# Layer 1's attention scores in split parts, with its side work set later, in a two-layer decoder trunk

## The chip, the cores and the metric

One core of a Trainium2 chip runs the whole program in one launch. The metric is the device time in microseconds (us), as the median over runs. TensorE is called PE here, as in the profile (PEld is its loading of weights), VectorE DVE, ScalarE ACT, GpSimd POOL and SyncE SP.

## The reference

A trunk of two layers on x of 256 tokens by 2048 features, in float32. Each layer is a token mixer and a gated MLP, each behind an RMS norm. Layer 0's mixer is attention in which every query attends causally to its own block of 256 keys; layer 1's is latent attention (MLA), and only that is changed:

```python
cq = rms_norm(h @ wq_a, g_qa)                       # rank 512
q = (cq @ wq_b).reshape(B, S, H, NOPE + RD)         # 16 heads of 128 + 64
q_nope = rms_norm(q[..., :NOPE], g_qn)
q_rope = rope(rms_norm(q[..., NOPE:], g_qr), pos, RD)
kv_a = h @ wkv_a
ckv = rms_norm(kv_a[..., :512], g_kva)
k_rope = rope(rms_norm(kv_a[..., 512:], g_kr), pos, RD)   # one for all heads
kv = (ckv @ wkv_b).reshape(B, S, H, NOPE + VD)
k_nope = rms_norm(kv[..., :NOPE], g_kn)
v = kv[..., NOPE:]
s = (q_nope @ k_nope.T + q_rope @ k_rope.T) * scale       # per head, causal
o = softmax(s) @ v
```

## The kernel before, in words

All weights stream once from HBM, in 1464 pieces of 128x512 (some 128x576). SP loads them four at a time into `raw`; ACT casts each to `whi` (fp32r) and DVE makes the remainder `wlo` = raw - whi (L111, L112). A product of two float32 operands is then three fp32r products: high by high, low by high, high by low. A plain float32 product is two passes on PE.

The program is a list of *quanta*, one for each weight piece: a quantum is the products of that piece, six of 128x512 where tokens are the rows (`tok_major`, L250), twelve of 128x256 where features are (`feat_major`, L276 to L278). The order is written out by hand: `at(q, f)` hangs side work behind the products of quantum q, `first_in` hangs work ahead of that. Each engine gets its instructions in the order of this list and runs them strictly in that order, except that PE loads weights ahead. At the start of quantum q the cast and the remainder of piece q + 3 are issued; `whi` and `wlo` have five buffers each.

Layer 1's attention takes four groups of four heads. Group 0 has its pieces in the order queries, rotary queries (second half), keys, values; groups 1 to 3 in the order keys, queries, values, four pieces each. The quanta of group 1 are 836 to 847, of group 2 848 to 859, of group 3 860 to 871; then the output projection begins. For queries and for keys a `Heads` object does, from the quantum q of the last piece on:

- `evac`: ACT copies both halves of the tokens from PSUM into a tile `qk` (two buffers in all)
- `squares`: DVE sums the squares of each head (L394); `rstd`: POOL takes the power -1/2
- `scaled`: DVE multiplies by it (L425); `turned`: PE transposes two heads (L473) into a tile `tp`, of which there are two in PSUM, shared with the probabilities' transposes
- `turned_out`: ACT copies `tp` with the gain into a part of a big tile `room` (L484)

Before, these stand at q, q+1 and q+2, q+3, q+5 and q+6, q+9 and q+10; and queries and keys have two places each in `room`, which takes the buffer of the norm's tile `h`.

A `Head` computes at its quantum the scores on PE: for the first 128 queries by the first 128 keys (columns 0 to 127 of a PSUM tile `sc`), and for the second 128 queries by all 256 keys. In layer 1 each is a plain float32 product (L510) followed by two fp32r products of the rotary parts (L515). In layer 0 (`parts=True`) the second product is in three fp32r products (`three`, L488 to L490), the first plain (L505). Then `biased` adds the mask and takes the maximum (DVE, L521), `exps` (ACT, L530) a quantum later, `normal` (DVE, L537, L539) two later, `turn` (PE, L547) and `turned` six later, `values` (PE, L572, L573) nine later. The heads of a group come three quanta apart, beginning 11 after the queries' (in group 0: keys') last piece.

The rotary queries of heads 8 to 15 (`rotary_queries(1, ...)`) are scaled, rotated in eight DVE steps and turned at offsets from quantum 827 given by a list.

Of the kernel before, what the change touches and what calls it, by code (L numbers as in the profile page):

```python
# [10 lines left out]
F32 = mybir.dt.float32  # L11
# [6 lines left out]
P = 128  # L18
# [32 lines left out]
BY_TOKEN, BY_FEATURE = (8, 8), (24, 56)  # L51

H_START = 8


class Stream:
# [66 lines left out]
def trunk(ctx: ExitStack, tc: tile.TileContext, a, out):  # L123
# [104 lines left out]
    def at(q, f, *args):  # L228
        side.setdefault(q, []).append((f, args))
# [51 lines left out]
    class Norm:  # L281
# [86 lines left out]
    class Heads:  # L368


        def __init__(self, state, n_heads, dh, gain, rot, tabs, scale, gain_column=None):
            self.gain_column = gain_column
# [26 lines left out]
        def squared(self):  # L399

            self.sq = []
            for t in range(NT):
                sq = att_pool.tile([P, 16 * 32], F32, name="ro2", bufs=2)
                nc.scalar.activation(sq, self.x[:, t].rearrange("p n d -> p (n d)"), AF.Square)
                self.sq.append(sq.rearrange("p (n d) -> p n d", n=self.n))

# [13 lines left out]
            nc.gpsimd.tensor_tensor(self.r, ms, mhalf[:, : NT * n], op=ALU.pow)  # L420

        def scaled(self, t):
            if self.gain_column is not None or self.gain is None:
                r = self.r[:, t * self.n : (t + 1) * self.n]
                nc.vector.tensor_tensor(  # L425
                    self.x[:, t], self.x[:, t], r[:, :, None].to_broadcast([P, self.n, self.dh]),
                    op=ALU.mult,
                )
                return
            g = gains[:, self.gain : self.gain + self.dh]  # L430
            for i in range(self.n):
                c = t * self.n + i
                nc.vector.scalar_tensor_tensor(
                    self.x[:, t, i], self.x[:, t, i], self.r[:, c : c + 1], g,
                    op0=ALU.mult, op1=ALU.mult,
                )
# [38 lines left out]
                    )  # L475
            pair["tp"] = tp

        def turned_out(self, dst, pair, i0):
            o = dst[:, i0 : i0 + 2, :].rearrange("p a s -> p (a s)")
            if self.gain_column is None:  # L480
                nc.scalar.copy(o, pair["tp"])
            else:
                c = self.gain_column
                nc.scalar.activation(o, pair["tp"], AF.Copy, scale=par[:, c : c + 1])  # L484

    def three(o, w_hi, w_lo, m_hi, m_lo, start, stop):

        mm(o, w_hi, m_hi, start=start, stop=False)  # L488
        mm(o, w_hi, m_lo, start=False, stop=False)  # L489
        mm(o, w_lo, m_hi, start=False, stop=stop)  # L490


    class Head:
# [4 lines left out]
        def scores(self):  # L498
            sc = ps_sc.tile([P, 512], F32, name="sc")
            qT, kT, i = self.qT(), self.kT(), self.i  # L500
            self.sc = sc
            if self.parts:

                (q0, q1), (k0, k) = qT, kT
                mm(sc[:, :P], q0[:, i], k0[:, i], start=True, stop=True)  # L505
                three(sc[:, P : 3 * P], q1[:, 0, i], q1[:, 1, i], k[:, 0, i], k[:, 1, i], True, True)
                return
            for q0, n, c in ((0, P, 0), (P, S, P)):
                o = sc[:, c : c + n]
                mm(o, qT[:, i, q0 : q0 + P], kT[:, i, :n], start=True, stop=self.rope is None)  # L510
                if self.rope is not None:

                    qr, kr = self.rope()
                    for part in range(2):
                        mm(o, qr[:, q0 : q0 + P], kr[:, part, :n], start=False, stop=part == 1)  # L515

        def biased(self):
            self.s = att_pool.tile([P, 3 * P], F32, name="s", bufs=3)
# [63 lines left out]
        def plan(self, q, q_values, q_turn=None):  # L582


            q_turn = q_turn or q + 6
            at(q, self.scores)
            at(q, self.biased)
            at(q + 1, self.exps)
            at(q + 2, self.normal)
            first_in(q_turn, 1, self.turn)  # L590
            first_in(q_turn, 1, self.turned)
            first_in(q_values, 0, self.values)
            first_in(q_values, 0, self.parted)
# [17 lines left out]
            att_pool.tile([P, 2, 512], F32R, name="v"), att_pool.tile([P, 512], F32, name="v1"),  # L611
        )

    def queries_out(dst, tp, i0):
# [4 lines left out]
        nc.scalar.copy(hi, src[:, :, 1])  # L619
        nc.scalar.copy(q0[:, i0 : i0 + 2], src[:, :, 0])  # L620
        nc.vector.tensor_tensor(lo, src[:, :, 1], hi.bitcast(F32), op=ALU.subtract)

    def keys_out(dst, tp, i0):

        k0, k = dst
        src = tp.rearrange("p (a s) -> p a s", a=2)
        hi, lo = k[:, 0, i0 : i0 + 2], k[:, 1, i0 : i0 + 2]
        nc.scalar.copy(hi, src)
        nc.scalar.copy(k0[:, i0 : i0 + 2], src[:, :, :P])
        nc.vector.tensor_tensor(lo, src, hi.bitcast(F32), op=ALU.subtract)  # L630

    def evac_parts(state, key, scale):
        v0, v1 = env[key]
# [14 lines left out]
            else:  # L648
                nc.scalar.activation(dst, src, AF.Copy, scale=scale()[:, t : t + 1])

    def plan_heads(q, hs, key, step, out=None, late=0, wide=False):

        at(q, hs.evac)
        if wide:
            for t in range(NT):
                for i in (0, 2):
                    at(q + 1 + 2 * t + i // 2, hs.squares, t, range(i, i + 2))
                at(q + 8 + t, hs.scaled, t)
            at(q + 5, hs.rstd)
            for i0 in (0, 2):  # L660
                pair = {}
                q1 = q + 11 + i0 // 2
                at(q1, lambda p=pair, i0=i0: hs.turned(env[key], p, i0))
                at(q1, lambda p=pair, i0=i0: hs.turned_out(env[key], p, i0))
            return
        for t in range(NT):
            at(q + step * (1 + t), hs.squares, t)
        at(q + step * 3, hs.rstd)
        for t in range(NT):
            at(q + step * (5 + t) + late * (1 + t), hs.scaled, t)  # L670
            at(q + step * (5 + t) + late * (2 + t), hs.rotate, t)
        for i0 in (0, 2):
            pair = {}
            q1 = q + step * 9 + i0 // 2 + 2 * late
            at(q1, lambda hs=hs, p=pair, i0=i0, key=key: hs.turned(env[key], p, i0))
            if out is None:
                at(q1, lambda hs=hs, p=pair, i0=i0, key=key: hs.turned_out(env[key], p, i0))
            else:
                at(q1, lambda p=pair, i0=i0, key=key: out(env[key], p["tp"], i0))

    at(-1, n1.scaled, 0)
    at(9, load_constants)
# [1 line left out]
    for g in range(4):  # L684
        for kind in "qkv":
# [13 lines left out]
            if kind == "v":  # L699
                at(q, evac_parts, state, ("v", g), lambda: n1.rstd)  # L700
                q_v = q
            else:
                hs = Heads(state, 4, P, G_Q if kind == "q" else G_K, 32, (tab, T_MC, T_MS), lambda: n1.rstd)
                plan_heads(q + (0 if g else 15 if kind == "q" else 9), hs, ("qT" if kind == "q" else "kT", g), 1,
                           queries_out if kind == "q" else keys_out, 1)
                q_k = q
        for i in range(4):
            hd = Head(
# [378 lines left out]
    at(q + 13, kr_turn)  # L1087

    def mla_tiles(g):
        i = 4 * (g % 2)  # L1090
        env["qT", g] = env["room"][:, i : 4 + i]
        env["kT", g] = env["room"][:, 8 + i : 12 + i]
        i = 4 * (g % 3)
        env["v", g] = env["room"][:, 16 + i : 20 + i].rearrange("p (t c) s -> p t (c s)", t=NT)

    for g in range(4):
        for kind in "kqv" if g else "qrkv":
            if kind == "r":
                rotary_queries(1, (6, 10, 12, 15, 16, 17, 18, 20, 21, 23, 24, 25, 26, 28, 40))
                continue  # L1100
            state = {}
            for kt in range(4):
# [3 lines left out]
            if kind == "v":  # L1106
                at(q, evac_values, state, ("v", g), None)
            else:
                q_q = q
                hs = Heads(state, 4, P, None, 0, None, (lambda: cq["scale"]) if kind == "q" else None,  # L1110
                           C_GQN if kind == "q" else C_GKN)
# [143 lines left out]
```

## Time and profile before

| | |
|---|---|
| median of 3 runs | 2088.53 us (2088.42 to 2088.66) |
| profiled execution: its own time | 2088.55 us |
| its span | 2086.5 us |
| mean granted PE clock | 1.00 |
| PE busy | 2079.9 us (100%) |
| PEld busy | 2012.3 us (96%) |
| DVE busy | 1406.8 us (67%) |
| ACT busy | 1133.2 us (54%) |
| mean HBM read | 186 GB/s |

The span runs from the first to the last instruction in the trace; the execution's own time has some 2 us around it. Matmuls overlap on PE, so the durations in the rows are longer than the distance of their starts: what a product costs is read from starts. "idle before" is how long an engine stood ahead of an instruction, and the arrow names what ended that.

### The profile page before, as it was taken

The numbers are of one execution on the slowest core, as the hardware profiler recorded it, in microseconds if no ns is written. First come the engines' busy times: TensorE is split into PE (matmuls) and PEld (weight loads), VectorE is DVE, ScalarE is ACT, GpSimd is POOL, SyncE is SP. The second block draws the span as 40 slices with busy tenths as digits, with TensorE's granted clock in tenths as the row PEclk, the third lists the DMA queues.
The fourth block names the chain that finished last, engine by engine and source line by source line (L and its number), as shares of the span: only waits on it lengthen the run. The fifth ranks groups of instructions, "written<-read, shape, count | busy, mean of one in ns | idle before, by whom it ended". The sixth has DMA issues, their size and how long they took to land.

```text
span 2086.5 us, 42075 instructions
## 1 busy us (share of the span) xinstructions
PE 2079.9 (100%) x16716; PEld 2012.3 (96%) x16716; DVE 1406.8 (67%) x3012; ACT 1133.2 (54%) x2199; POOL 46.1 (2%) x35
## 2 busy tenths in 40 slices
PE   9999999999999999999999999999999999999999
PEld 7888889999999999999999889999999999999999
DVE  6777776776666766655556886776676666755554
ACT  6555555555555555545455666655555555544443
POOL 0000000000000000000000110000000000000000
PEclk9999999999999999999999999999999999999999
DMA  7454445455555555555554533555555555555553
GB/s 270 166 182 173 168 164 200 185 192 192 199 187 201 188 196 197 190 200 187 199 202 152 202 122 122 183 201 185 200 192 192 200 187 200 190 200 210 196 206 132
DMA packets 59381, 391.81 MB, mean 188 GB/s; under 512 B 6960, under 2 KB 9648, under 8 KB 13360
## 3 DMA queue, kind: packets, MB, share of 16 engines
q1 hardware_dynamic: 59040, 389.10, 52.6%
q8 instruction: 130, 2.13, 0.4%
q14 instruction: 67, 0.55, 0.1%
q10 hardware_dynamic: 144, 0.04, 0.0%
HBM read 387.01 MB, written 2.10 MB: 186 GB/s over the span
## 4 chain that ended last, share of the span: by engine, by line
PE 99%; DMA 0%; SPq 0%; DVE 0%; ACT 0%; issue 0%
PE acc L276 26%; PE acc L277 26%; PE acc L278 26%; PE acc L250 17%; PE tp L473 1%; PE sc L510 1%; PE tp L547 1%; PE sc L572 0%; PE sc L515 0%; DMA xT<-in_xT 0%; PE sc L489 0%; PE sc L490 0%; PE sc L488 0%; PE sc L570 0%; PE sc L505 0%; PE sc L573 0%
## 5 line engine op out<-in xcount | busy, mean ns | idle before, releaser
L112 DVE TENSOR_TENSOR wlo<-raw,whi 128x512 fp32r<-128x512 f32 (+1 forms) x1464 | 999.4, 689 | 390.1 <-ACT whi L111 387.5
L111 ACT CAST whi<-raw 128x512 fp32r<-128x512 f32 (+1 forms) x1463 | 869.2, 619 | 455.9 <-PE acc L277 212.5
L276 PE MATMUL acc<-h,whi 128*128 128x256 f32 x2880 | 795.4, 276 | 0.0
L278 PE MATMUL acc<-h,wlo 128*128 128x256 f32 x2880 | 794.9, 276 | 0.0
L277 PE MATMUL acc<-h,whi 128*128 128x256 f32 x2880 | 794.9, 276 | 0.0
L277 PEld LDWEIGHTS acc<-h,whi 128*128 128x128 f32 x2880 | 540.6, 188 | 0.0
L276 PEld LDWEIGHTS acc<-h,whi 128*128 128x128 f32 x2880 | 540.6, 188 | 0.0
L278 PEld LDWEIGHTS acc<-h,wlo 128*128 128x128 f32 x2880 | 540.5, 188 | 0.0
L276 PE MATMUL acc<-a,whi 128*128 128x256 f32 x1408 | 388.6, 276 | 0.0
L277 PE MATMUL acc<-a,whi 128*128 128x256 f32 x1408 | 388.6, 276 | 0.0
L278 PE MATMUL acc<-a,wlo 128*128 128x256 f32 x1408 | 388.6, 276 | 0.0
L250 PE MATMUL acc<-whi,h 128*128 128x512 f32 (+1 forms) x896 | 272.1, 379 | 1.9 <-DVE whi L109 1.3
L276 PEld LDWEIGHTS acc<-a,whi 128*128 128x128 f32 x1408 | 264.3, 188 | 0.0
L277 PEld LDWEIGHTS acc<-a,whi 128*128 128x128 f32 x1408 | 264.3, 188 | 0.0
L278 PEld LDWEIGHTS acc<-a,wlo 128*128 128x128 f32 x1408 | 264.3, 188 | 0.0
L250 PEld LDWEIGHTS acc<-whi,h 128*128 128x128 f32 x896 | 164.8, 188 | 31.7 <-issue 1.8
L250 PE MATMUL acc<-wlo,h 128*128 128x512 f32 (+1 forms) x448 | 168.5, 376 | 0.2 <-DVE wlo L112 0.2
L276 PE MATMUL acc<-oT,whi 128*128 128x256 f32 x512 | 142.6, 278 | 0.0
L278 PE MATMUL acc<-oT,wlo 128*128 128x256 f32 x512 | 141.6, 277 | 0.0
L277 PE MATMUL acc<-oT,whi 128*128 128x256 f32 x512 | 141.5, 276 | 0.0
L782 DVE TENSOR_TENSOR g<-acc,rstd_b 128x256 f32<-128x256 f32 x88 | 37.5, 426 | 125.4 <-PE acc L278 122.5
L789 ACT ACTIVATE c<-g,par 128x256 f32<-128x256 f32 x88 | 53.1, 603 | 108.3 <-DVE g L782 108.3
(163 smaller groups left out, 1598.4 us busy)
## 6 DMA issues: line engine op xcount, KB each, us to landing
raw<-in_ffn_gu SPq DMA_DIRECT2D x176, 1024.0 KB, 4.8
raw<-in_ffn_down SPq DMA_DIRECT2D x88, 1024.0 KB, 4.8
raw<-in_moba_wk SPq DMA_DIRECT2D x16, 1024.0 KB, 4.8
raw<-in_moba_wv SPq DMA_DIRECT2D x16, 1024.0 KB, 4.8
raw<-in_moba_wo SPq DMA_DIRECT2D x16, 1024.0 KB, 4.8
raw<-in_mla_wo SPq DMA_DIRECT2D x16, 1024.0 KB, 4.8
raw<-in_moba_wq SPq DMA_DIRECT2D x12, 1024.0 KB, 4.8
raw<-in_mla_wkv_a SPq DMA_DIRECT2D x8, 576.0 KB, 3.7
```

What stands on the lines that cost most here:

```text
L111: self.nc.scalar.copy(hi[:, :n], w)
L112: self.nc.vector.tensor_tensor(lo[:, :n], w, hi[:, :n].bitcast(F32), op=ALU.subtract)
L250: mm(state["acc"][t][:, :n], src[:, kt, c : c + P], (t_lo if part == 1 else t_hi)[:, :n], start=kt == 0 and part == 0, stop=kt == k_last a ...
L276: mm(o, w_hi, src[:, kt, :S], start=first and k == 0, stop=False, skip_group_check=True)
L277: mm(o, w_hi, src[:, kt, S:], start=False, stop=False, skip_group_check=True)
L278: mm(o, w_lo, src[:, kt, :S], start=False, stop=kt == k_last, skip_group_check=True)
L473: nc.tensor.transpose(tp[:, (i * NT + t) * P : (i * NT + t + 1) * P], flat[:, t, c : c + P], ident)
L510: mm(o, qT[:, i, q0 : q0 + P], kT[:, i, :n], start=True, stop=self.rope is None)
L547: nc.tensor.transpose(tp[:, c * P : (c + 1) * P], self.s[:, c * P : (c + 1) * P], ident)
L782: nc.vector.tensor_tensor(self.g[:, 2:], self.gate["acc"][:, :S], self.norm.rstd_b, op=ALU.mult)
L789: nc.scalar.activation(self.c, self.g[:, 2:], AF.Identity, bias=par[:, cb : cb + 1], scale=self.cw(2))
```

## The change

Layer 1 gets layer 0's form of the scores: the second half of the queries by all keys as three fp32r products, the first half by the first keys plain, and then the four rotary products on top of both (`skip_group_check` lets two groups of sums be open in one PSUM tile). Queries and keys are copied out with their gain as `(q0, q1)` and `(k0, k)`: a plain copy of the first half, and a high part (ACT) and a remainder (DVE) of the rest. The tile `h` becomes two tiles, `h0` and `h1`; in layer 1's attention their buffers hold `room` and `rparts`. Queries and keys have one place each there instead of two.

For layer 1's `Heads`, squares are taken by ACT into a tile `sq` and summed by DVE's reduction, and the steps stand at: evacuation q, squares q+1, sums q+3 and q+4, rstd q+4, scaling q+6 and q+7, turns q+9 and q+12 for queries, q+10 and q+14 for keys (group 0: q+11 and q+12, q+9 and q+10; its queries' rstd is at q+5, the scaling at q+8 and q+9). In layer 1 the exponentials come two quanta after the scores instead of one, and normalising four instead of two (for the last head: one and three). The rotary list is spread: the eight steps lie at 18 to 32 instead of 17 to 26, the turns at 35 and 41 instead of 28 and 40. Layer 0's work is as before, except for where the tiles lie.

```diff
+class Halves:
+    def __getitem__(self, at):
+        p, k, s = at
+        return self.tiles[k // 8][p, k % 8, s]
...
-                t = keep.tile([P, KD * 2 * S + 64], F32R, name="h")
-                self.h = t[:, H_START : H_START + KD * 2 * S].rearrange("p (k s) -> p k s", k=KD)
+                n = KD // 2 * 2 * S
+                tiles = [keep.tile([P, n + 64], F32R, name=f"h{i}") for i in range(2)]
+                self.h = Halves([
+                    t[:, H_START : H_START + n].rearrange("p (k s) -> p k s", k=KD // 2) for t in tiles
+                ])
...
         def scores(self):
-            for q0, n, c in ((0, P, 0), (P, S, P)):
-                o = sc[:, c : c + n]
-                mm(o, qT[:, i, q0 : q0 + P], kT[:, i, :n], start=True, stop=self.rope is None)
-                if self.rope is not None:
-                    qr, kr = self.rope()
-                    for part in range(2):
-                        mm(o, qr[:, q0 : q0 + P], kr[:, part, :n], start=False, stop=part == 1)
+            (q0, q1), (k0, k) = qT, kT
+            first_, second = sc[:, :P], sc[:, P : 3 * P]
+            last = self.rope is None
+            flags = {} if last else {"skip_group_check": True}
+            mm(first_, q0[:, i], k0[:, i], start=True, stop=last, **flags)
+            three(second, q1[:, 0, i], q1[:, 1, i], k[:, 0, i], k[:, 1, i], last, last, **flags)
+            if last:
+                return
+            qr, kr = self.rope()
+            for o, t, n in ((first_, 0, P), (second, 1, S)):
+                for part in range(2):
+                    mm(o, qr[:, t * P : (t + 1) * P], kr[:, part, :n],
+                       start=False, stop=part == 1, **flags)
...
         def plan(self, q, q_values, q_turn=None):
-            at(q + 1, self.exps)
-            at(q + 2, self.normal)
+            late = self.rope is not None
+            at(q + 1 + (late and q_turn == q + 6), self.exps)
+            at(q + 2 + late + (late and q_turn == q + 6), self.normal)
...
+    def copied(dst, src, gain):            # ACT copy, with the gain as scale
+    def rest_of(lo, src, hi, gain):        # DVE: src * gain - hi
-    def keys_out(dst, tp, i0):
+    def keys_out(dst, tp, i0, gain=None):
         k0, k = dst
         src = tp.rearrange("p (a s) -> p a s", a=2)
         hi, lo = k[:, 0, i0 : i0 + 2], k[:, 1, i0 : i0 + 2]
-        nc.scalar.copy(hi, src)
-        nc.scalar.copy(k0[:, i0 : i0 + 2], src[:, :, :P])
-        nc.vector.tensor_tensor(lo, src, hi.bitcast(F32), op=ALU.subtract)
+        copied(hi, src, gain)
+        copied(k0[:, i0 : i0 + 2], src[:, :, :P], gain)
+        rest_of(lo, src, hi, gain)
...
     def open_room():
-        t = keep.tile([P, KD * 2 * S + 64], F32, name="room", tag="h")
-        env["room"] = t[:, : 32 * S].rearrange("p (k s) -> p k s", k=32)
+        n = KD // 2 * 2 * S
+        t = keep.tile([P, n + 64], F32, name="room", tag="h0")
+        env["room"] = t[:, :n].rearrange("p (k s) -> p k s", k=n // 512)
+        t = keep.tile([P, n + 64], F32R, name="rparts", tag="h1")
+        env["rparts"] = t[:, H_START : H_START + 3072].rearrange("p (k s) -> p k s", k=6)
...
+    def plan_latent(q, hs, key, out, sums, rest, turns):
+        at(q, hs.evac)
+        at(q + 1, hs.squared)
+        for t in range(NT):
+            at(q + sums + t, hs.sums, t)
+            at(q + rest + (2 if rest < 5 else 3) + t, hs.scaled, t)
+        at(q + rest, hs.rstd)
+        for i0, turn in zip((0, 2), turns):
+            pair = {}
+            at(q + turn, lambda p=pair, i0=i0: hs.turned(None, p, i0))
+            at(q + turn, lambda p=pair, i0=i0: out(env[key], p["tp"], i0))
...
-                rotary_queries(1, (6, 10, 12, 15, 16, 17, 18, 20, 21, 23, 24, 25, 26, 28, 40))
+                rotary_queries(1, (6, 10, 12, 15, 16, 18, 20, 22, 24, 26, 28, 30, 32, 35, 41))
...
-                plan_heads(q, hs, ("qT" if kind == "q" else "kT", g), 1, wide=(g, kind) == (0, "q"))
+                c, put, turns = (
+                    (C_GQN, queries_out, (9, 12)) if kind == "q" else (C_GKN, keys_out, (10, 14))
+                )
+                if g == 0:
+                    turns = (11, 12) if kind == "q" else (9, 10)
+                plan_latent(
+                    q, hs, ("qT" if kind == "q" else "kT", g), with_gain(put, c), 3,
+                    5 if (g, kind) == (0, "q") else 4, turns,
+                )
```

More of the change, by code (lines that the diff above doesn't have):

```diff
@@ L53, with __init__ @@
 H_START = 8
+class Halves:
+    def __init__(self, tiles):
+        self.tiles = tiles
+    def __getitem__(self, at):
+        p, k, s = at
+        return self.tiles[k // 8][p, k % 8, s]
 class Stream:
@@ L476, in turned, with three @@
             pair["tp"] = tp
[L478 to L490, printed above, removed]
+    def three(o, w_hi, w_lo, m_hi, m_lo, start, stop, **flags):
+        mm(o, w_hi, m_hi, start=start, stop=False, **flags)
+        mm(o, w_hi, m_lo, start=False, stop=False, **flags)
+        mm(o, w_lo, m_hi, start=False, stop=stop, **flags)
     class Head:
@@ L612, in moba_tiles, with queries_out @@
         )
[L614 removed]
+    def copied(dst, src, gain):
+        if gain is None:
+            nc.scalar.copy(dst, src)
+        else:
+            nc.scalar.activation(dst, src, AF.Copy, scale=gain)
+    def rest_of(lo, src, hi, gain):
+        if gain is None:
+            nc.vector.tensor_tensor(lo, src, hi.bitcast(F32), op=ALU.subtract)
+        else:
+            nc.vector.scalar_tensor_tensor(
+                lo, src, gain, hi.bitcast(F32), op0=ALU.mult, op1=ALU.subtract
+            )
+    def queries_out(dst, tp, i0, gain=None):
         q0, q1 = dst
@@ L649, in evac_values, with plan_heads @@
                 nc.scalar.activation(dst, src, AF.Copy, scale=scale()[:, t : t + 1])
-    def plan_heads(q, hs, key, step, out=None, late=0, wide=False):
+    def plan_heads(q, hs, key, out):
         at(q, hs.evac)
[L654 to L665, printed above, removed]
         for t in range(NT):
-            at(q + step * (1 + t), hs.squares, t)
-        at(q + step * 3, hs.rstd)
+            at(q + 1 + t, hs.squares, t)
+        at(q + 3, hs.rstd)
         for t in range(NT):
-            at(q + step * (5 + t) + late * (1 + t), hs.scaled, t)
-            at(q + step * (5 + t) + late * (2 + t), hs.rotate, t)
+            at(q + 6 + 2 * t, hs.scaled, t)
+            at(q + 7 + 2 * t, hs.rotate, t)
         for i0 in (0, 2):
             pair = {}
[L674 to L679, printed above, removed]
+            q1 = q + 11 + i0 // 2
+            at(q1, lambda hs=hs, p=pair, i0=i0: hs.turned(None, p, i0))
+            at(q1, lambda p=pair, i0=i0, key=key: out(env[key], p["tp"], i0))
     at(-1, n1.scaled, 0)
```

47 lines of the change are left out of this document (27 added, 20 removed).

## The prediction

> **What bounds the kernel now.** I read the page first: span, busy shares, and the chain that ended last.
>
> ```profile
> span 2086.5 us, 42075 instructions
> PE 2079.9 (100%) x16716; PEld 2012.3 (96%) x16716; DVE 1406.8 (67%) x3012; ACT 1133.2 (54%) x2199; POOL 46.1 (2%) x35
> PE 99%; DMA 0%; SPq 0%; DVE 0%; ACT 0%; issue 0%
> ```
>
> TensorE (PE) is busy all the time and 99% of the chain is PE. So a product taken off PE shortens the run by its own time, and other engines cost nothing until PE waits for them. Next I asked whether that holds in layer 1's attention, with the windows view over the twelve quanta of head group 1 and of group 2 (a quantum is one weight piece with its six products and the side work hung on it).
>
> ```profile
> core 0: us, PE busy (x) PEld busy (x) DVE busy (x) ACT busy (x) POOL busy (x), PEclk, DMA share, GB/s
> 1197.85:1222.86 25.01, 25.01 (x140) 21.54 (x139) 22.59 (x87) 17.90 (x44) 3.89 (x2) 1.00 0.38 129
> 1222.86:1250.01 27.15, 27.15 (x155) 23.49 (x153) 23.50 (x96) 19.85 (x49) 3.89 (x2) 1.00 0.33 123
> ```
>
> PE is full at granted clock 1.00. VectorE (DVE) is busy 22.59 of 25.01 and 23.50 of 27.15 us, so it has 2.4 and 3.7 us to spare; ScalarE (ACT) has over 7. DVE is the engine that could take over.
>
> **Term 1, the scores on PE.** PE's timeline over one head of layer 1, then over one head of layer 0, which already has the form that layer 1 gets:
>
> ```profile
> 1241.79 0.39 PE L510 MATMUL sc<-room 128*128 128x128 f32 x2
> 1241.93 0.42 PE L515 MATMUL sc<-kr,qrT 128*128 128x128 f32 x2
> 1242.18 0.65 PE L510 MATMUL sc<-room 128*128 128x256 f32 x2
> 1242.48 0.59 PE L515 MATMUL sc<-kr,qrT 128*128 128x256 f32 x2
> 1242.90 0.40 PE L250 MATMUL acc<-whi,cqT 128*128 128x512 f32 x1
> ...
> 146.08 0.38 PE L505 MATMUL sc<-k,q 128*128 128x128 f32 x2
> 146.22 0.36 PE L488 MATMUL sc<-k,q 128*128 128x256 f32 x1
> 146.42 0.28 PE L489 MATMUL sc<-k,q 128*128 128x256 f32 x1
> 146.53 0.28 PE L490 MATMUL sc<-k,q 128*128 128x256 f32 x1
> 146.65 0.40 PE L250 MATMUL acc<-whi,h 128*128 128x512 f32 x1
> ```
>
> A head now takes 1242.90 - 1241.79 = 1.11 us up to the next weight product: each f32 product is two passes. The new form is layer 0's block, 146.65 - 146.08 = 0.57 us, and then the same four rotary products. One of 256 columns takes 146.53 - 146.42 = 0.11; one of 128 columns I take as a transpose of that size:
>
> ```profile
> 1218.94 0.60 PE L473 MATMUL tp<-ident,qk 128*128 128x128 f32 x4
> 1219.30 0.47 PE L250 MATMUL acc<-whi,cqT 128*128 128x512 f32 x1
> 1220.76 0.59 PE L572 MATMUL sc<-pT,room 128*128 128x256 f32 x2
> 1221.41 0.49 PE L547 MATMUL tp<-ident,s 128*128 128x128 f32 x3
> 1224.25 0.60 PE L473 MATMUL tp<-ident,qr 128*128 128x128 f32 x4
> ```
>
> Three starts apart, less one duration of 0.27: (0.60 - 0.27) / 3 = 0.11. So 0.57 + 4 x 0.11 = 1.01 us, a saving of 0.10 a head, or 0.09 within the rounding of these starts; I take 0.09, times 16 heads = **-1.4 us**. Bounds: were a 128-column product half of a 256-column one, 0.11 more a head, -3.2 us; were each head to pay one more change of form like the 0.20 between L488 and L489 instead of 0.11, nothing is left, 0. I take -1.4, the rows being of the very forms.
>
> The Trainium skill ("TensorE: Matmul & The Clock Gate", section "Wait — 56ns, not 53.3ns?") puts a warm product at its columns over 2.4 GHz plus about 2.5 ns, 56 ns at 128 columns; by that the sum of this term would be an estimated -3.1 us. The trace has 0.11 us at 128 columns.
>
> **Term 2, the load on DVE and ACT.** Per group, DVE loses 16 sums of squares (L394) and gains 4 reductions (as L408), 2 remainders of queries (as L941) and 2 of keys (as L638):
>
> ```profile
> L394 DVE CUSTOM_DVE_ANT_0 junk<-qk 128x128 f32<-128x128 f32 x128 | 29.7, 286 | 0.0
> L408 DVE TENSOR_REDUCE ss<-ro 128x8 f32<-128x512 f32 x4 | 2.7, 680 | 0.0
> L638 DVE SCALAR_TENSOR_TENSOR v<-acc,rstd,v 128x512 fp32r<-128x512 f32 x4 | 3.0, 744 | 0.0
> L941 DVE SCALAR_TENSOR_TENSOR ckvT<-tp,par,ckvT 128x256 fp32r<-128x256 f32 x4 | 1.9, 485 | 0.5 <-ACT ckvT L940 0.2
> ...
> 1209.70 0.15 DVE L537 RECIPROCAL sst<-sst 128x2 f32<-128x2 f32 x1
> 1210.35 0.68 DVE L112 TENSOR_TENSOR wlo<-raw,whi 128x512 fp32r<-128x512 f32 x1
> ```
>
> By busy time over count that is -16 x 0.23 + 4 x 0.68 + 2 x 0.48 + 2 x 0.75 = +1.5 us at most. The rotary stages, put further apart, move three of eight steps out of group 1 into group 2, one of 128x512 (0.68 as L112's in the timeline) and two of half that: 1.4 us. Group 2 then asks 23.5 + 1.5 + 1.4 = 26.4 of 27.15 - 4 x 0.09 = 26.8 us. ACT gains four squares of 128x512 and a few copies a group, with 7 us to spare. So on average nothing becomes the bound, and the finer spread takes away the two quanta in which eight sums of squares pile up. I cost the load, the exponentials and normalising set a quantum later, and the later rotary turns at nothing; the cover is this slack on DVE (0.4 us in group 2), which is thin; the price if it is gone is the second rival's.
>
> **Term 3, a wait that the change adds.** The tile `qk`, into which queries and keys are evacuated, has two buffers. In the changed order the second pair of keys is turned 14 quanta after the evacuation instead of 10, while the next use of that buffer, by the keys of the group after, comes 12 quanta after. So at quantum 851 (last key piece of group 2; 863 for group 3) ACT's evacuation waits for PE's transposes at the end of quantum 853 (865): two quanta ahead of it. The instruction order of the changed kernel shows it: these are the only two such waits in layer 1, and there is none before. Queued behind it on ACT are the casts of pieces 855 and 856 and the copies of the queries turned at 852, on which DVE's remainder waits, for which the next probabilities' transposes on PE wait, since they take the same `tp` buffer. ACT's timeline gives the prices, DVE's rows stand above:
>
> ```profile
> 1212.44 0.40 ACT L530 ACTIVATE s<-s,sst 128x128 f32<-128x128 f32 x1 [1.23 <-DVE sst L526]
> 1213.33 0.67 ACT L484 ACTIVATE room<-tp,par 128x512 f32<-128x512 f32 x1
> 1215.56 1.08 ACT L387 COPY qk<-acc 128x512 f32<-128x512 f32 x2
> 1216.52 0.65 ACT L111 CAST whi<-raw 128x512 fp32r<-128x512 f32 x1
> ...
> 1173.96 0.47 ACT L940 ACTIVATE ckvT<-tp,par 128x256 fp32r<-128x256 f32 x1 [0.63 <-PE tp L935]
> 1174.33 1.26 ACT L389 ACTIVATE qr<-acc,cscale 128x512 f32<-128x512 f32 x2
> 1175.47 1.16 ACT L404 ACTIVATE ro<-qr 128x512 f32<-128x512 f32 x2
> 1176.51 2.18 ACT L111 CAST whi<-raw 128x512 fp32r<-128x512 f32 x4
> ```
>
> The evacuation at 1215.56 moves behind the transposes of 853, which end at 1218.94 + 0.60 = 1219.54: ACT stands for 4.0 us. From there (t = 0): two evacuations 0.96 (1216.52 - 1215.56), the cast of 855 ending at 0.96 + 0.65 = 1.61 and letting the next one start after 0.51 ((2.18 - 0.65) / 3, four casts in a row), at 1.47, then the queries' high part and copy at 0.37 (1174.33 - 1173.96) and 0.47, done at 2.31. DVE, after the cast: remainder of the weights 0.6 up to the next start, reciprocal and normalising 0.65 (1209.70 to 1210.35), so 1.61 + 1.25 = 2.86, then the queries' remainder 0.48: done at 3.3. PE, undisturbed, wants its transposes at 1221.41 - 1219.54 = 1.87. **First stall: 1.5 us**, counting handovers of some 0.04.
> Then ACT: from 2.2, two squares 1.04 (1176.51 - 1175.47), the cast of 856 0.51, exponentials 0.89 (1213.33 - 1212.44), keys' high part 0.57 and copy 0.47: done at 5.7; keys' remainder on DVE 0.74: 6.5. PE wants the `tp` buffer for the second pair of queries, now at 855, at 1224.25 - 1219.54 - 0.09 + 1.5 = 6.1. **Second stall: 0.4 us.** After that the probabilities' transposes of 857 find their operand some 0.1 us ahead, by the same count, and those of 860 as well; the weight pieces are in time throughout, because three are cast ahead. So 1.9 us a group, two groups: **+3.8 us**. Bounds: 0, if the first stall is covered by something that the count misses; and 2 x 4.0 = 8.0 us, if PE loses all that ACT stands.
>
> **The rest.** Splitting `h` lets no instruction wait longer, and moves every tile behind its first half by 256 bytes; I cost that at nothing, since the products of layer 0 and of layer 1 above, on tiles at quite other places, keep one pace (0.11 us), and leave the doubt to the last rival.
>
> **The sum.** The profiled execution took 2088.55 us for a span of 2086.5; the runs' median is 2088.53. 2088.5 - 1.4 + 3.8 = **2090.9 us**, 0.11% slower. A measurement of this kernel can tell about 0.2% (4.2 us) from no change, so this counts as within it.
>
> **Rivals.** *The wait is hidden* (0.13): ACT's stand costs PE nothing, and only term 1 is left, 2087.1 us. For it: PE has its pieces to 854 cast when ACT stops. Against it: the shared `tp` buffer, which the count finds 1.5 us late.
> *The backlog isn't worked off* (0.18), the slower side: after each stand DVE, with 0.4 us of slack in group 2, stays one 128x512 instruction (0.6 us) later than counted, and the turns of 857 and 860, with 0.1 us in hand, wait too: 2 turns x 2 groups x 0.6 = +2.4, 2093.3 us. It decides as soon as DVE is more than 0.1 us later than my count. Against it: ACT has slack, and group 3 has less rotary work.
> ```profile
> L530 ACT ACT_TABLE_LOAD x1 | 1.3, 1283 | 0.0
> ```
>
> *Table loads* (0.01): 16 squares now stand between exponentials. If each change of function loaded a table (1.28 us by this row), five pairs would bring ten loads, and two of the pairs lie in the catch-up with two loads each: 2 x 2 x 1.28 = +5.1, 2096.0 us. Against it: this is the first exponential after layer 0's MLP, and the load is made once though squares and exponentials both follow; the changed order has no more loads. The Trainium skill ("ScalarE: Activation LUTs", section "Table sets: the hidden batching unit") holds that functions come in sets and that a change of set costs a load; the row speaks for one set here.
> *Addresses or something unseen* (0.04): a pace other by 0.3% would be 6 us either way.
>
> **How the numbers follow.** Forecast 0.64, rivals 0.13, 0.18, 0.01, 0.04. The forecast's own range is 2089.0 to 2092.5 (a stall of 2 to 5.4 us). The range that holds 8 in 10 takes in the hidden wait and most of the backlog: 2087.0 to 2093.6. Faster by over 0.2% needs under 2084.4, half of the unseen: 0.02. Slower by over 0.2% needs above 2092.7: most of the backlog (0.13), the loads, half of the unseen, a tail of the forecast (0.03): 0.19. Within: 0.79.
>
> **What would show it.** Right: PE idle of about 1.5 us before transposes of `s` and 0.4 us before transposes of `qk`, in groups 2 and 3 only; ACT's idle of some 4 us twice before the copy to `qk`, ended by PE; heads 0.09 us shorter. Wrong: no PE idle there (then 2087), waits at more places than these four (then 2093 and above), or another pace of products outside layer 1's attention.

## The result, and the profile after

The changed kernel takes 2092.99 us (median of 13 runs, 2092.29 to 2093.48) against 2088.53 us before (13 runs, 2088.31 to 2088.89): 4.46 us more, ratio 1.0021 with a 95% interval of 1.0014 to 1.0029. That is a small slowdown. It lies just above the 2092.7 us from which the prediction called the change slower, an outcome to which it gave 0.19; the interval takes in 0.2%. The forecast was 2090.9 us in a range of 2087.0 to 2093.6. The profiled execution took 2093.38 us.

The page of the changed kernel, its span, busy times and the chain:

```profile
span 2091.3 us, 42059 instructions
PE 2082.0 (100%) x16732; PEld 2013.4 (96%) x16732; DVE 1411.7 (68%) x2916; ACT 1145.5 (55%) x2231; POOL 45.7 (2%) x35
PE 98%; ACT 1%; DVE 0%; DMA 0%; issue 0%; SPq 0%; ACTq 0%
```

PE is on 98% of the chain instead of 99%, and ACT has 1%. The windows over the same twelve quanta each as before show where. (The prediction calls these two stretches groups 1 and 2; they are the quanta 843 to 854 and 855 to 866, seven later than the pieces of those groups.)

```profile
core 0: us, PE busy (x) PEld busy (x) DVE busy (x) ACT busy (x) POOL busy (x), PEclk, DMA share, GB/s
1198.18:1225.41 27.23, 24.76 (x140) 20.98 (x138) 22.35 (x62) 19.24 (x46) 3.90 (x2) 1.00 0.27 94
1225.41:1254.27 28.86, 27.31 (x159) 23.30 (x158) 24.68 (x68) 22.56 (x57) 3.89 (x2) 1.00 0.33 110
```

They last 27.23 and 28.86 us instead of 25.01 and 27.15, and PE, full before, stands 2.47 and 1.55 us in them. DVE is busy 22.35 and 24.68 us, so it is not full on average; the clock is 1.00 as before. What PE waited for, from the waits of the changed kernel (engine, line, what it waited for: sum in us, times, longest):

```profile
ACT qk L400 <- PE tp L486: 7.1, 2, 4.2
PEld tp L556 <- DVE rparts L636: 3.2, 2, 1.6
PE tp L556 <- DVE rparts L636: 2.8, 2, 1.4
PEld tp L486 <- DVE rparts L636: 1.1, 2, 0.6
PE tp L556 <- DVE s L548: 1.0, 1, 1.0
```

The first row is the new forward wait (L400 is the evacuation into `qk`, L486 the transposes of `qk`); the next three are its effect, two turns of probabilities (L556) and two of queries, all behind the remainder `rparts` (L636). The last is a wait that the prediction did not have: a turn behind the normalising (L548).

To price each, the start of every quantum's first weight product is set against that of the kernel before; a step in this difference is time won or lost there. Steps that every kernel shows without a wait (0.08 us won a head, 0.35 us where four transposes have moved from one quantum to another) are taken off. The difference over the whole stretch, quanta 833 to 888, is +4.4 us and stays flat from there to the end. Up to 833 the two traces differ by 0.4 us, and the variants below by -0.9 to +0.3, so the prediction's last rival, another pace outside layer 1's attention, does not show. The parts of the 4.4 us: 2.0 us at 854 and 855, 2.0 at 866 and 867, 1.3 at 848, 0.3 at 872, 0.1 at 880, less the heads.

PE's timeline over one head of the changed kernel:

```profile
1224.37 0.39 PE L513 MATMUL sc<-room 128*128 128x128 f32 x2
1224.51 0.36 PE L493 MATMUL sc<-rparts 128*128 128x256 f32 x1
1224.71 0.28 PE L494 MATMUL sc<-rparts 128*128 128x256 f32 x1
1224.83 0.28 PE L495 MATMUL sc<-rparts 128*128 128x256 f32 x1
1224.94 0.63 PE L521 MATMUL sc<-kr,qrT 128*128 128x128 f32 x4
1225.41 0.40 PE L261 MATMUL acc<-whi,cqT 128*128 128x512 f32 x1
```

1.04 us instead of 1.11. Over the 16 heads, from the first score's start to the next product of another kind, the sum falls from 17.90 to 16.63 us: -1.27. With the waits, -1.27 + 2.0 + 2.0 + 1.3 + 0.3 + 0.1 = 4.4 us.

The forward wait and its first two effects, from the timeline of the changed kernel:

```profile
1219.92 0.60 PE L486 MATMUL tp<-ident,qk 128*128 128x128 f32 x4
1222.17 0.38 PE L582 MATMUL sc<-pT,room 128*128 128x128 f32 x2
1223.98 0.55 PE L556 MATMUL tp<-ident,s 128*128 128x128 f32 x3 [1.43 <-DVE rparts L636]
1227.09 0.66 PE L486 MATMUL tp<-ident,qk 128*128 128x128 f32 x4
...
1222.18 0.69 DVE L123 TENSOR_TENSOR wlo<-raw,whi 128x512 fp32r<-128x512 f32 x1 [2.78 <-ACT whi L122]
1222.79 0.16 DVE L546 RECIPROCAL sst<-sst 128x2 f32<-128x2 f32 x1
1223.45 0.48 DVE L636 SCALAR_TENSOR_TENSOR rparts<-tp,par,rparts 128x256 fp32r<-128x256 f32 x1
1226.28 0.75 DVE L636 SCALAR_TENSOR_TENSOR rparts<-tp,par,rparts 128x512 fp32r<-128x512 f32 x1 [0.53 <-ACT room L629]
...
1220.56 1.07 ACT L400 COPY qk<-acc 128x512 f32<-128x512 f32 x2 [4.19 <-PE tp L486]
1221.52 0.63 ACT L122 CAST whi<-raw 128x512 fp32r<-128x512 f32 x1
1222.40 0.48 ACT L629 ACTIVATE room<-tp,par 128x256 f32<-128x256 f32 x1
```

ACT stands 4.19 us until the transposes of 853 have ended (1219.92 + 0.60). Its cast comes late, DVE stands 2.78 us for that, and all that DVE has behind it, the queries' remainder last, ends at 1223.45 + 0.48 = 1223.93; PE starts the turn at 1223.98. The second turn starts at 1227.09, when the keys' remainder of 1226.28 has ended.

In the next group the same evacuation stands less long, since ACT had a cast of rotary queries to do until 1246.5:

```profile
1249.41 1.07 ACT L400 COPY qk<-acc 128x512 f32<-128x512 f32 x2 [2.93 <-PE tp L486]
```

PE loses 2.0 us there all the same. What counts is when the stand ends, behind PE's transposes, and not how long it is.

### The profile page after: what moved, and what is told of

The parts are those of the page before. It is cut to its first block, busy times and chain, and to the rows that moved or that the text cites. A ratio compares the mean times of both kernels' runs of the same rounds, so it can differ in the third digit from the quotient of the medians.

```text
span 2091.3 us, 42059 instructions
## 1 busy us (share of the span) xinstructions
PE 2082.0 (100%) x16732; PEld 2013.4 (96%) x16732; DVE 1411.7 (68%) x2916; ACT 1145.5 (55%) x2231; POOL 45.7 (2%) x35
## 4 chain that ended last, share of the span: by engine, by line
PE 98%; ACT 1%; DVE 0%; DMA 0%; issue 0%; SPq 0%; ACTq 0%
PE acc L287 26%; PE acc L289 26%; PE acc L288 26%; PE acc L261 17%; PE tp L486 1%; PE tp L556 0%; PE sc L513 0%; PE sc L581 0%; PE sc L521 0%; PE sc L493 0%; PE sc L494 0%; PE sc L495 0%; DMA raw<-in_moba_wq 0%; ACT whi L122 0%; PE sc L579 0%; ACT sq L417 0%
```

## The experiments

Four theories were to be told apart: the buffer of `qk` (the prediction's term 3), DVE simply too full (its second rival), something at the first head (the wait on L548), and the size of the scores' saving. The table gives for each kernel the median, that of the kernel before on the same chip, and in the single trace the waits at four places and the difference over quanta 833 to 888, worked out as above (us). Medians of the kernel before differ by up to 0.3 us between the groups of runs, so two kernels of different groups are compared by the column "less before". The 95% interval of each ratio to before is some 0.0009 either way, 1.8 us; smaller differences rest on the steps in the traces, which agree with the medians within 0.3 us.

| kernel | median | before | less before | 848 | 852-855 | 863-867 | 872 | 833-888 |
|---|---|---|---|---|---|---|---|---|
| changed | 2092.99 | 2088.53 | +4.46 | 1.3 | 2.0 | 2.0 | 0.3 | +4.4 |
| third buffer | 2088.64 | 2088.43 | +0.21 | 1.3 | 0 | 0 | 0.3 | +0.4 |
| early softmax | 2095.42 | 2088.43 | +6.99 | 0 | 4.8 | 3.1 | 0 | +7.3 |
| both | 2092.24 | 2088.43 | +3.81 | 0 | 2.0 | 2.4 | 0 | +3.9 |
| third buffer, load early | 2088.02 | 2088.62 | -0.60 | 0.5 | 0 | 0 | 0.3 | -0.4 |
| third buffer, squares later | 2087.38 | 2088.62 | -1.24 | 0.3 | 0 | 0 | 0 | -1.0 |
| third buffer, normalising at three | 2087.59 | 2088.70 | -1.11 | 0 | 0.3 | 0 | 0 | -0.9 |
| third buffer, squares on DVE | 2089.22 | 2088.62 | +0.60 | 1.1 | 0 | 0 | 0.3 | +0.7 |
| three repairs | 2087.08 | 2088.36 | -1.28 | 0.2 | 0 | 0 | 0 | -1.0 |

**1. A third buffer for `qk`.**

```diff
-                self.x = att_pool.tile([P, NT, n, dh], F32, name="qk", bufs=2)
+                self.x = att_pool.tile([P, NT, n, dh], F32, name="qk", bufs=2 if self.gain is not None else 3)
-                r = att_pool.tile([P, 16 * 32], F32, name=name, bufs=2)
+                r = att_pool.tile([P, 16 * 32], F32, name=name, bufs=1 if rot == 64 and name == "ro1" else 2)
-                junk = att_pool.tile([P, 512], F32, name="kvjunk", tag="ro1", bufs=2)
+                junk = att_pool.tile([P, 512], F32, name="kvjunk", tag="sq", bufs=2)
```

> The changed kernel with three buffers for qk in layer 1 instead of two (room comes from one buffer for ro1, and kvjunk in the buffers of sq). No instruction changes place on any engine; only the evacuation's wait for PE's later transposes goes, and addresses in that pool. Theory A, the buffer: the stalls before 854, 855, 866 and 867 (1.6, 0.3, 1.6, 0.3 us) go, and with them what is left of the backlog at 872 (0.4 us); the stall before the first head's transposes at 848 (1.4 us) stays: 2093.0 - 3.8 to 4.2 = 2088.8 to 2089.2 us. Rival B, the vector engine is simply too full in groups 2 and 3 and the wait is only where that shows: the remainder is late without the wait too, at least half of the stalls stay: 2091 us or above.

2088.64 us (ratio to before 1.0001, 0.9992 to 1.0009): by the column "less before" 4.25 us less than the changed kernel, by the traces 4.0. From its waits, what is left of the five rows above:

```profile
PE tp L556 <- DVE s L548: 1.0, 1, 1.0
ACT qk L400 <- PE acc L261: 0.9, 1, 0.9
```

The evacuation no longer waits for transposes, and all four waits for `rparts` are gone, though DVE has the same instructions in the same order. So the buffer costs 4.0 us, and DVE is not too full. The wait at 872 stayed, so it was not backlog, as the expectation had it.

**2. The exponentials and the normalising where the kernel before has them.**

```diff
-            at(q + 1 + (late and q_turn == q + 6), self.exps)
-            at(q + 2 + late + (late and q_turn == q + 6), self.normal)
+            at(q + 1, self.exps)
+            at(q + 2, self.normal)
```

> The changed kernel with the exponentials one quantum and the normalising two quanta after the scores again, as in the kernel before; nothing else changes. Theory A: the stall of 1.4 us before the first head's transposes at 848 comes of the later normalising, which meets the table load and two squares on ScalarE; it goes, the four stalls at 854 to 867 stay: 2093.0 - 1.4 = 2091.6 us. Rival B: the table load and the squares delay VectorE's queue whatever the order, so the normalising is as late as it was: 2093.0 us. Rival C: normalising early stands in the way of weight remainders or of the remainders of queries and keys, stalls elsewhere grow: above 2093.5 us.

2095.42 us: rival C. The waits at 848 and 872 do go, but those at 852 to 855 and 863 to 867 grow by 2.8 and 1.1 us, and a new one of 0.6 us comes at 876, which the table has no column for (nor for the next run, where it is the same).

**3. Both edits together.**

> The third buffer and the early exponentials and normalising together. Theory A, two separate causes, their gains add: 2093.0 - 3.8 - 1.4 = 2087.8 us, or 2087.4 if the stall of 0.4 us at 872 goes too; less than the kernel before by 0.7 to 1.1 us, which is what the scores alone save (1.4) less what is left. Rival B, one cause seen at two places, or VectorE is too full: the gains don't add, 2089 us or above.

2092.24 us, 3.6 us above the third buffer alone: the gains do not add. From the timeline of this kernel at quantum 852:

```profile
1217.73 0.44 PE L486 MATMUL tp<-ident,qk 128*128 128x128 f32 x2 [1.01 <-DVE qk L438]
...
1214.46 0.75 DVE L636 SCALAR_TENSOR_TENSOR rparts<-tp,par,rparts 128x512 fp32r<-128x512 f32 x1 [1.05 <-ACT room L629]
1216.99 0.68 DVE L438 TENSOR_TENSOR qk<-qk,hr 128x512 f32<-128x512 f32 x1
...
1212.51 0.41 ACT L539 ACTIVATE s<-s,sst 128x128 f32<-128x128 f32 x1 [2.27 <-DVE sst L535]
```

Issued a quantum earlier, the exponentials reach ACT before DVE has made the bias `sst`: ACT stands 2.27 us, with the keys' copies queued behind. DVE then stands 1.05 us for those copies, the keys are scaled late (1216.99), and PE stands 1.01 us for that. The later exponentials of the change, which the prediction put at nothing, save this. The edit also moves the normalising, and no run moves the exponentials alone, so that the exponentials are the cause is read from these rows.

**4. The second half of the scores as one plain product again,** on the changed kernel, and **5.** the same with the third buffer.

```diff
-            three(second, q1[:, 0, i], q1[:, 1, i], k[:, 0, i], k[:, 1, i], last, last, **flags)
+            if last:
+                three(second, q1[:, 0, i], q1[:, 1, i], k[:, 0, i], k[:, 1, i], last, last, **flags)
+            else:
+                mm(second, q1[:, 0, i].bitcast(F32), k[:, 0, i].bitcast(F32), start=True, stop=False, **flags)
```

> The changed kernel, but the second half of layer 1's scores is one f32 product of the high parts (128 by 256, two passes), as the kernel before did it, in place of three fp32r products; the low parts are still made but not used. Theory A: the three products save 0.085 us a head, so 16 heads cost 16 x 0.085 = 1.4 us more: 2094.4 us, or some 0.2 less where the longer scores cover a piece of a stall; each head's scores take 1.11 us again. Rival B: the shorter heads only move idle time, PE waits that much longer later: 2093.0 us.

> The third buffer, with the second half of layer 1's scores as one f32 product of the high parts (the low parts' products are left out), as in the earlier run of that edit, but without the four stalls that could swallow a piece of it. Theory A: a head's scores take 1.11 instead of about 1.02 us and all of it is on the path: 16 x 0.085 = +1.4, less up to 0.2 swallowed at 848 and 872: 2089.8 to 2090.0 us. Rival B: as on the changed kernel only 0.7 us shows, because the products save less than the heads' times say: 2089.3 us.

2093.65 us (before 2088.43), 0.76 us more than the changed kernel by "less before" and 0.7 by the traces. With the third buffer it is 2089.82 us (before 2088.62), 1.0 more than the third buffer alone by both. In both traces the 16 heads sum to 17.9 us again, as in the kernel before. So of the 1.27 us by which the heads are shorter, 1.0 shows in the time when the four waits for the remainder are gone: the median meets theory A, the difference lies between the two theories. The steps from quantum to quantum show where most of the rest is. Behind a head that is longer by 0.08 us, the next wait is shorter by as much: once each at 848 and 872, and in the changed kernel also at 854 and 855 and at 866 and 867. And behind each of the last five heads 0.03 us comes back in the next quantum.

**6. The table load ahead of the first head,** with the third buffer.

```diff
+    def early_table():
+        t = att_pool.tile([P, 1], F32, name="pre", tag="kro1")
+        nc.scalar.activation(t, mhalf[:, :1], AF.Exp)
+    at(q + 12, early_table)
```

> The third buffer, and one exponential of a 128x1 column some 20 quanta ahead of layer 1's first head, so that the table is loaded there. Theory A: of ScalarE's work between the first head's scores and its transposes at 848, the load (1.28 us) is what is on the path: the cast behind it, for which VectorE stood 1.25 us, comes 1.28 us earlier, the normalising too, and the stall of 1.3 us at 848 goes: 2088.6 - 1.3 = 2087.3 us; the 0.3 us at 872 stays. Rival B: the squares and the rest of ScalarE's queue alone make it late, or the normalising a quantum later does: the stall keeps half or more, 2088.0 us or above.

2088.02 us, by "less before" and by the traces 0.8 less than the third buffer alone; the wait at 848 falls from 1.3 to 0.5 us. From the timeline of this kernel:

```profile
1206.99 0.61 PE L556 MATMUL tp<-ident,s 128*128 128x128 f32 x3 [0.26 <-DVE s L548]
...
1203.19 0.69 DVE L123 TENSOR_TENSOR wlo<-raw,whi 128x512 fp32r<-128x512 f32 x1 [0.47 <-ACT whi L122]
```

DVE's stand ahead of the cast's remainder shrinks from 1.25 to 0.47 us, no further, since the squares are still ahead of the cast, the second of them standing 0.51 us for one of DVE's sums (L421). The median lies just on the border that rival B had (2088.0), the wait is under half of what it was: neither theory is met in full.

**7. The squares a quantum later,** with the third buffer.

```diff
-        at(q + 1, hs.squared)
+        at(q + 2, hs.squared)
```

> The third buffer, and ScalarE's two squares of queries and keys two quanta after the evacuation instead of one (behind the cast that they delay now). Theory A: at 848 and at 872 the squares (1.04 us) stand between the exponentials and the cast for which VectorE stands (1.25 and 1.46 us); with the cast ahead of them the stall at 848 shrinks from 1.3 to about 0.3 us and the one at 872 (0.3 us) goes: 2088.6 - 1.3 = 2087.3 us. Rival B: the squares then delay the exponentials or the copies of the next quantum by the same 1.04 us, and new stalls come in their place: 2088.6 us or above.

2087.38 us: theory A. ACT's timeline of this kernel now has the cast ahead of the squares, and DVE, which no longer stands, reaches the normalising in time but for 0.3 us; at 872 nothing waits:

```profile
1202.93 0.61 ACT L122 CAST whi<-raw 128x512 fp32r<-128x512 f32 x1
1203.44 1.15 ACT L417 ACTIVATE sq<-qk 128x512 f32<-128x512 f32 x2
```

**8. The sums of squares on DVE again,** with the third buffer.

```diff
-        at(q + 1, hs.squared)
         for t in range(NT):
-            at(q + sums + t, hs.sums, t)
+            at(q + 1 + t, hs.squares, t)
```

> The third buffer, with the sums of squares of queries and keys on VectorE again, eight each in the two quanta behind the evacuation, as the kernel before has them (room from the squares' own buffers). Theory A: VectorE is the engine without slack; it gets 16 x 0.23 - 4 x 0.68 = 1.0 us more a group, in lumps of 0.9 us, ahead of the normalising: ScalarE's freed 1.04 us doesn't help, the stall at 848 stays about 1.3 us, and new stalls come in groups 2 and 3: 2089.5 to 2091 us. Rival B: ScalarE's squares are the reason for both stalls; they go: 2087.0 us.

2089.22 us, by "less before" 0.4 above the third buffer alone, and below the expected 2089.5. The waits at 848 and 872 stay (1.1 and 0.3 us) and one of 0.5 us comes at 840; groups 2 and 3, where the expectation had the new ones, show none. Having the squares on ACT is worth 0.4 us here, which is little.

**9. Three repairs together:** the third buffer, the squares later, the load early.

> The third buffer, the squares a quantum later and the early table load together. Theory A: PE waits nowhere in layer 1's attention any more but for what the kernel before has too; only the scores' saving is left: the kernel before less 1.2 to 1.4 us, 2087.1 to 2087.4 us, 0.0 to 0.3 us below the run with the squares later. Rival B: the two repairs of 848 get in each other's way, or the load where it now stands delays a cast: 2088 us or above.

2087.08 us (2086.64 to 2087.51; before on the same chip 2087.87 to 2089.15), ratio 0.9994 with an interval of 0.9985 to 1.0003. The chain of this kernel is PE's again, and its span 1.4 us below that of before:

```profile
span 2085.1 us, 42062 instructions
PE 99%; DMA 0%; SPq 0%; DVE 0%; ACT 0%; issue 0%
```

With the next one it is the fastest kernel of the study; no run of it was as long as the shortest of before beside it, but the interval does not exclude 1.

**10. Two buffers, but the second keys turned earlier,** with the other two repairs.

```diff
-                    (C_GQN, queries_out, (9, 12)) if kind == "q" else (C_GKN, keys_out, (10, 14))
+                    (C_GQN, queries_out, (9, 12)) if kind == "q" else (C_GKN, keys_out, (10, 12))
```

> The same with two buffers for qk again, and the second pair of keys turned 12 instead of 14 quanta after the evacuation: then no evacuation waits for transposes of a later quantum. Theory A: it is the wait on a later quantum that costs, not the number of buffers: 2087.1 to 2087.6 us, as with three buffers. Rival B: with two buffers ScalarE's evacuation still stands until the end of the quantum, and the transposes come into a quantum in which the keys aren't scaled or the tp buffer isn't free: 2089 us or above.

2087.11 us (before 2088.36): theory A, as good as the third buffer, without its memory. What costs is a turn set 14 quanta after an evacuation whose buffer is wanted after 12.

**11. The rotary steps at their old quanta,** on the three repairs.

```diff
-                rotary_queries(1, (6, 10, 12, 15, 16, 18, 20, 22, 24, 26, 28, 30, 32, 35, 41))
+                rotary_queries(1, (6, 10, 12, 15, 16, 17, 18, 20, 21, 23, 24, 25, 26, 28, 40))
```

> The three repairs, with layer 1's second rotary work at the quanta of the kernel before instead of the wider spread. Theory A: VectorE has over 2 us to spare in group 1, so the spread is worth nothing there or up to 0.3 us: 2087.1 to 2087.5 us. Rival B: three more steps in group 1 (1.4 us of VectorE) meet the sums, the scaling and the remainders, and PE waits: 2088 us or above.

2087.59 us (before 2088.36), 0.5 above: between the two theories. The trace has 0.3 us more wait at 848 and none at 855 and 867, and over quanta 833 to 888 it is only 0.2 us longer. So the spread saves 0.2 to 0.5 us; the prediction had it at nothing.

**12. The normalising at three quanta,** with the third buffer.

```diff
-            at(q + 2 + late + (late and q_turn == q + 6), self.normal)
+            at(q + 2 + late, self.normal)
```

> The third buffer, with the normalising three quanta after the scores instead of four; the exponentials stay at two. Theory A: the stalls of 1.3 us at 848 and 0.3 us at 872 come of the normalising being set two quanta later than in the kernel before, behind the next head's bias, a scaling and a remainder (1206.07 to 1208.02 in the changed kernel's trace, some 2 us): one quantum back they go, 2088.6 - 1.6 = 2087.0 us. Rival B: an earlier normalising stands ahead of the keys' scaling or remainder, as with the early exponentials (+3.6 us there), and PE waits for those: above 2088.6 us.

2087.59 us, by "less before" and by the traces 1.3 below the third buffer alone: theory A for 848 and 872. From its timeline:

```profile
1207.21 0.49 PE L556 MATMUL tp<-ident,s 128*128 128x128 f32 x3
1207.53 0.39 PE L513 MATMUL sc<-room 128*128 128x128 f32 x2
...
1206.02 0.55 DVE L548 TENSOR_SCALAR s<-s,sst 128x128 f32<-128x128 f32 x2
```

The probabilities are ready 0.6 us ahead of the turn. It costs 0.3 us at 852, so it gains 1.3 and not the whole 1.6.

## Why the prediction was right, and where not

**The number.** 2092.99 us lies in the stated range, but not in the forecast's own part of it, 2089.0 to 2092.5. It is nearest to the 2093.3 of the second rival, the backlog, which did not come: the range was wide enough for that rival, and a term that the forecast had left out filled it. So the number fell in the range partly by luck. Of the signs that the prediction named, those of being right came (PE idle at the four places, ACT's stand twice, shorter heads), and one of being wrong came as well: waits at more places than these four, with a time of 2093.

**Right: the scores.** Forecast -1.4 us, measured -1.27 by the heads' starts; 1.0 of it shows in the time of runs 5 and 1. The count of 1.01 us a head was short by 0.03. From the 56 ns that the Trainium skill ("TensorE: Matmul & The Clock Gate", section "Wait — 56ns, not 53.3ns?") gives for a product of 128 columns, the prediction estimated -3.1 us; the trace does not agree. The four rotary products take 1225.41 - 1224.94 = 0.47 us, 0.12 each, at 128 columns as at 256, and the row decides.

**Right: the new wait.** Forecast 1.5 and 0.4 us in each of two groups, +3.8; measured 1.65 and 0.35, +4.0, and run 1 takes it away alone. The steps held too: ACT's stand 4.19 for 4.0 (the second, also put at 4, is 2.93); the queries' copy done 2.32 us after the evacuation's start for 2.31 (1222.40 + 0.48 - 1220.56); the remainder done at 3.37 for 3.3; the keys' remainder at 6.47 for 6.5.

**Right: the rivals that were refused.** The wait was not hidden. The backlog was worked off: the turns of 857 and 860 do not wait in the trace. No second table load came.

**Wrong: the term costed at nothing.** "I cost the load, the exponentials and normalising set a quantum later, and the later rotary turns at nothing; the cover is this slack on DVE (0.4 us in group 2)". Two mistakes lie in it. The normalising is set two quanta later, not one, and the cover was looked for in an average over the second stretch (855 to 866), while the place is the first head, in the stretch before it. The kernel before there:

```profile
1207.18 0.49 PE L547 MATMUL tp<-ident,s 128*128 128x128 f32 x3
...
1203.02 0.55 DVE L539 TENSOR_SCALAR s<-s,sst 128x128 f32<-128x128 f32 x2
```

The normalising ended at 1203.57 and had 3.6 us in hand. The changed kernel at the same place:

```profile
1208.64 0.61 PE L556 MATMUL tp<-ident,s 128*128 128x128 f32 x3 [1.04 <-DVE s L548]
1209.09 0.39 PE L513 MATMUL sc<-room 128*128 128x128 f32 x2
...
1204.85 0.69 DVE L123 TENSOR_TENSOR wlo<-raw,whi 128x512 fp32r<-128x512 f32 x1 [1.25 <-ACT whi L122]
1206.07 0.28 DVE L530 CUSTOM_DVE_ANT_0 s<-sc,mask 128x128 f32<-128x128 f32 x1
1208.21 0.55 DVE L548 TENSOR_SCALAR s<-s,sst 128x128 f32<-128x128 f32 x2
...
1200.99 1.28 ACT L539 ACT_TABLE_LOAD   x1
1203.17 1.14 ACT L417 ACTIVATE sq<-qk 128x512 f32<-128x512 f32 x2
1204.22 1.65 ACT L122 CAST whi<-raw 128x512 fp32r<-128x512 f32 x3
```

The normalising is at 1208.21, 5.2 us later than before by these two rows, of which 0.3 is the distance of the two traces (1198.18 and 1197.85 at the start of 843). The next head's bias (from 1206.07 on), a scaling and a remainder now stand ahead of it, some 2 us; and ACT has load, exponentials and squares ahead of the cast for which DVE stands 1.25 us. All 3.6 us in hand go, and 1.3 more. Any one of three edits takes away most of it: one quantum back (run 12, all), the squares behind the cast (run 7, 1.0), the load earlier (run 6, 0.8). At 872 the same happens for 0.3 us without a load, and runs 7 and 12 take that away too. This 1.6 us and 0.1 at 880 are what the forecast lacks; the 0.2 us that the buffer's wait is larger and the 0.1 that the scores save less make up the rest of 2093.0 - 2090.9.

The load itself was over-counted: the second stretch was to ask 26.4 us of DVE; it asks 24.68. So the average slack was larger than thought, and it still covered nothing at 848. That the later exponentials and the wider rotary spread gain, 3.6 us (runs 1 and 3, together with the normalising) and 0.2 to 0.5 us (run 11), was not foreseen either; the first is a gain only within the changed order, since in the kernel before PE does not wait for its earlier exponentials.

Open: the 0.1 us at 880, which every variant shows, and why 0.03 us comes back behind each of the last heads.

## What to carry to other kernels

When a step is moved by whole quanta on an engine that runs in order, read at each of its instances how long its result lay ready before the reader took it, and what is queued ahead of it at the new place; a stretch's mean slack says nothing of that. List, for each tile with rotating buffers, the distance from its filling to its last reader, and compare it with the distance to the filling that takes the same buffer: a reader two quanta too late cost three times what the change saved, and one number in a list repairs it. Take each part of a mixed change apart on the chip: here one part was worth -1.3 us, one +4.0, one +1.6, and one that looked like only a delay held off 3.6.

## What the runs showed of the hardware

In these traces a block of transposes that had to wait costs more than its wait. The three of 848 take 0.45 us to the next product in the changed kernel (1208.64 to 1209.09 in the rows above), those of 854 take 0.39 (1223.98 to 1224.37), and the three of 848 take 0.32 where they did not wait (1207.21 to 1207.53 with the normalising at three). So 0.06 to 0.13 us came on top of the idle time that the waits list; why is not shown.
